# Product-key experts: 144 tokens gathered and 368 dense, with blocks of V as the stationary operand

## The chip, the core and the metric

The kernel runs on one core of one Trainium2 chip. The metric is the device time of one execution in microseconds (us), as the median of several runs. Engines are named as in the profile: PE (TensorE matmul), PEld (its weight load), DVE (VectorE), ACT (ScalarE), POOL (GpSimd) and SP (SyncE, which issues DMAs).

## The reference

One layer of a hybrid encoder block on 512 tokens of width 2048: a combined projection, neighbourhood attention beside a bidirectional RWKV-7 mixer, an output projection, and then an expert network. What matters here is the last part, all in float32:

```python
q = (u @ w_q).reshape(T, 8, 256)                       # u: the normed residual x, T = 512
s1, s2 = q[..., :128] @ sub_k1.T, q[..., 128:] @ sub_k2.T
# per head: the 16 best pairs of 128 x 128 keys -> 16 of 16384 experts, gate = softmax of their scores
hidden = gelu(einsum('cd,chkd->chk', u, exp_u[ec])) * gate      # exp_u, exp_v: 16384 x 2048
out = einsum('chk,chkd->cd', hidden, exp_v[ec])                 # 8 x 16 = 128 picks per token
x = x + gate2 * out
```

## The kernel before

The stages run one after the other: front and mixer, attention and merge (to about 1900 us), `out_proj`, `peer_select`, then `Experts.form` and `Experts.main`, which fill the time from about 2300 us to the end.

**Two ways to the experts.** For the first 128 tokens (`TS`) the kernel gathers: token t sits on partition t, and for each of its 128 picks `Picks` fetches one row of U and one of V per token (1 MB per fetch, an indirect DMA from POOL's queue into one of three `row` buffers). A row of U gives a dot product with the token (`L1221` on DVE), a row of V is added to `y3` (`L1229` on DVE). For the other 384 tokens (`TD`) the kernel computes all 16384 experts densely: U times tokens, Gelu, times a gate that is zero for experts not picked, times V.

**The dense part.** An expert tile is 128 experts. A U unit multiplies 16 blocks of U^T (128x128) with the token columns. Every float32 product is made of three float32r matmuls (`mm3`): high part of the weights by high and by low part of the tokens, low part of the weights by the high part. So a U unit is 48 matmuls of 384 columns. `Experts.spill` stores every fourth expert tile's result (32 tiles) in the forming stage; the main stage makes the other 96. A group is four expert tiles: six U steps (three units of two steps) and then eight V steps. In a V step the gated activations H are the stationary operand, 128 tokens at a time, and V streams by 512 columns: 3 token tiles x 2 expert tiles x 3 parts = 18 matmuls of 512 columns (`L1457` to `L1459`); two steps fill three PSUM tiles of [128 tokens, 512], which DVE adds to `ys` (`L1378`).

**The weight stream.** Each step needs one tile of 128x1024 weights. SP loads it into `raw` (`L1284`, two buffers), ACT casts it to the high part `wh` (`L496`), and DVE, or POOL for every `k.lp`-th tile, subtracts to get the low part `wl` (`L498`, in `w_split`); the step's matmuls follow two steps later. Here and elsewhere a helper makes the instruction, and the profile then names its line, L131: look for the tile.

**The gates.** In the forming stage `Gates` builds, in sets of 8 tokens, the gate of every expert for every dense token, and POOL stores them to `G` in blocks of 32 tokens. The main stage reads them back per group (`gt`, from SP's queue, the first from POOL's), and POOL multiplies them into the activations (`gated`, `L1352`). With `gt` a spilled tile (`ge<-gel`) is loaded.

**What sets the order.** From `form` on, each engine runs its instructions in the order in which the program writes them: per step first the split and load for two steps on, then what is late from the last unit (H parts), the unit's end (additions, gating), the matmuls, and at the end of each unit as many picks as the pace asks for. POOL's queue thus holds, in this order, gate multiplications and row fetches, and each fetch waits until DVE is done with the row it replaces.

Of the kernel before, what the change touches and what calls it, by code (L numbers as in the profile page):

```python
# [448 lines left out]
TS = 128  # L449
TD = 512 - TS  # L450
NT = TD // 128
# [546 lines left out]
def out_proj(k, tc):  # L998
    nc = k.nc
    V, A, G, T = nc.vector, nc.scalar, nc.gpsimd, nc.tensor  # L1000
    with tc.tile_pool(name="x2", reuse_waits="tile", bufs=1) as xp, tc.tile_pool(name="psE", reuse_waits="tile", bufs=1, space=PSUM) as pp:
# [5 lines left out]
        for d in range(16):  # L1007
# [31 lines left out]
        for kt in range(16):  # L1039
# [6 lines left out]
            if kt % 4 == 0:  # L1046
                pt = pp.tile([128, 512], F32, name="acc3", bufs=4)
            T.transpose(pt[:TS, (kt % 4) * 128:(kt % 4 + 1) * 128], x[:, :TS], k.c["I"])
            if kt % 4 == 3:
                A.copy(k.u3[:TS, (kt - 3) * 128:(kt + 1) * 128], pt[:TS])  # L1050


def peer_select(k, tc, pq, psF):
# [45 lines left out]
    for t in range(4):  # L1099
# [22 lines left out]
        if t == 0:  # L1122
            flat = lambda a: a[:TS].rearrange("p h n -> p (h n)")
            V.tensor_copy(k.g3[:TS], flat(sel[0]))
            V.scalar_tensor_tensor(k.idx3[:TS], flat(sel[1]), 128.0, flat(sel[2]), ALU.mult, ALU.add)
        if t < TS // 128:
            continue
        for i in range(3):
            p = psF.tile([128, 512], F32, name="sp", bufs=2)
            T.transpose(p[:, :128], sel[i].rearrange("p h n -> p (h n)"), k.c["I"])  # L1130
            A.copy(k.selT[i][:, t * 128 - TS:t * 128 + 128 - TS], p[:, :128])


class Gates:
# [35 lines left out]
    def keep(self, g):  # L1170
        if 0 <= g < self.n:
# [5 lines left out]
            if q == 3:  # L1177
                k.nc.gpsimd.dma_start(k.G[g // 4], self.st)

# [7 lines left out]
class Picks:  # L1187
# [4 lines left out]
    def __init__(self, k):  # L1192
        self.k, self.items, self.fetched, self.at = k, [], [], 0
        nb = 128 // self.BATCH
        for b in range(nb + 1):
            js = lambda i: [(i, j) for j in range(self.BATCH * (b - i), self.BATCH * (b - i + 1))]
            dots, adds = js(0) if b < nb else [], js(1) if b else []
            mix = [x for p in zip(dots, adds) for x in p] if dots and adds else dots + adds
            self.items += mix

    def fetch(self):
        k, n = self.k, len(self.fetched)
        if n < len(self.items):
            kind, j = self.items[n]
            t = k.rows.tile([128, D], F32, name="row", bufs=k.rb)
            k.nc.gpsimd.indirect_dma_start(out=t, out_offset=None, in_=k.i[("un", "vn")[kind]],  # L1206
                                           in_offset=bass.IndirectOffsetOnAxis(ap=k.idx3[:, j:j + 1], axis=0))
            self.fetched.append(t)

    def step(self):  # L1210
# [3 lines left out]
        V, A = k.nc.vector, k.nc.scalar  # L1214
# [360 lines left out]
def lay_out(i):  # L1575
# [3 lines left out]
    r = {}  # L1579
# [65 lines left out]
```

## Time and profile before

| | |
|---|---|
| runs (three) | median 4622.17 us, from 4617.81 to 4643.67 |
| the profiled execution | 4636.11 us, its span 4634.3 us |
| mean granted clock of TensorE in it | 0.969 of full speed |
| HBM | read 889.22 MB, written 88.08 MB |
| DMA queues | SP's 662.05 MB, POOL's 315.38 MB |

Busy times below are of that one execution. Matmuls are pipelined, so their durations (389 ns median for 512 columns) overlap; their pace is the distance between starts. A wait is put down to what came last; idle time of an engine that is not the bottleneck costs nothing.

### The profile page before, as it was taken

The numbers are of one execution on the slowest core, as the hardware profiler recorded it, in microseconds if no ns is written. First come the engines' busy times: TensorE is split into PE (matmuls) and PEld (weight loads), VectorE is DVE, ScalarE is ACT, GpSimd is POOL, SyncE is SP. The second block draws the span as 40 slices with busy tenths as digits, with TensorE's granted clock in tenths as the row PEclk, the third lists the DMA queues.
The fourth block names the chain that finished last, engine by engine and source line by source line (L and its number), as shares of the span: only waits on it lengthen the run. The fifth ranks groups of instructions, "written<-read, shape, count | busy, mean of one in ns | idle before, by whom it ended". The sixth has DMA issues, their size and how long they took to land.

```text
span 4634.3 us, 63846 instructions
## 1 busy us (share of the span) xinstructions
PE 4392.5 (95%) x23633; PEld 3724.2 (80%) x23633; DVE 3195.8 (69%) x4854; ACT 1757.6 (38%) x3368; POOL 1549.6 (33%) x1322
## 2 busy tenths in 40 slices
PE   6979999999999989998989999999999999999999
PEld 5757777777776777787889998888888888898887
DVE  8856665556552766546897767777777777777777
ACT  4532445454434443334246633222322232322332
POOL 4236344444432312232233322222222232322223
PEclk9989999999989989998999999999999999999999
DMA  9765344434432747652246777877777777787785
GB/s 327 245 228 162 121 132 130 114 114 117 120 86 78 263 159 243 232 182 79 91 147 244 246 261 284 283 265 282 279 269 279 279 269 283 275 287 283 270 291 170
DMA packets 371305, 981.52 MB, mean 212 GB/s; under 512 B 82416, under 2 KB 134512, under 8 KB 336432
## 3 DMA queue, kind: packets, MB, share of 16 engines
q1 hardware_dynamic: 325968, 662.05, 44.1%
q0 software_dynamic: 45024, 315.38, 18.2%
q8 instruction: 186, 3.05, 0.3%
q14 instruction: 127, 1.04, 0.1%
HBM read 889.22 MB, written 88.08 MB: 211 GB/s over the span
## 4 chain that ended last, share of the span: by engine, by line
PE 52%; DMA 18%; DVE 13%; issue 4%; ACT 4%; POOL 2%; SPq 2%; ACTq 0%; POOLq 0%; DVEq 0%
PE acc L131 35%; DMA raw<-pv 8%; DMA raw<-pu 6%; DVE wl L131 4%; PE pm L131 4%; PE acc L1459 3%; PE acc L1457 3%; ACT wh L131 3%; PE acc L1458 3%; PE us L131 2%; PE xo L131 2%; DMA adaw<-ada 1%; DVE row L1221 1%; DMA TT<-sQ 1%; PE pg L1168 1%
## 5 line engine op out<-in xcount | busy, mean ns | idle before, releaser
L131 PE MATMUL acc<-X,wh 128*128 128x384 f32 (+1 forms) x7680 | 2242.4, 369 | 23.6 <-ACT wh L131 12.8
L131 PEld LDWEIGHTS acc<-X,wh 128*128 128x128 f32 x7680 | 1413.4, 190 | 172.7 <-ACT wh L131 15.9
L131 ACT CAST wh<-raw 128x1024 fp32r<-128x1024 f32 (+1 forms) x952 | 836.0, 880 | 1691.4 <-DMA raw<-pv 557.9
L131 PE MATMUL acc<-X,wl 128*128 128x384 f32 (+1 forms) x3840 | 1418.7, 370 | 13.4 <-DVE wl L131 10.2
L131 DVE TENSOR_TENSOR wl<-raw,wh 128x1024 fp32r<-128x1024 f32 (+1 forms) x644 | 781.0, 1214 | 623.6 <-ACT wh L131 614.2
L131 PEld LDWEIGHTS acc<-X,wl 128*128 128x128 f32 x3840 | 727.8, 190 | 91.1 <-DVE wl L131 15.9
L131 POOL TENSOR_TENSOR wl<-raw,wh 128x512 fp32r<-128x512 f32 (+1 forms) x308 | 477.6, 1553 | 770.8 <-ACT wh L131 707.3
L1457 PE MATMUL acc<-wh,H 128*128 128x512 f32 x1536 | 604.7, 394 | 31.8 <-ACT wh L131 17.7
L1459 PE MATMUL acc<-wl,H 128*128 128x512 f32 x1536 | 604.6, 394 | 6.9 <-DVE wl L131 6.6
L1458 PE MATMUL acc<-wh,H 128*128 128x512 f32 x1536 | 602.3, 392 | 2.7 <-DVE H L521 2.7
L1206 POOL DMA_INDIRECT row<-un,idx x128 | 184.6, 1442 | 634.3 <-DVE y L1229 575.1
L1457 PEld LDWEIGHTS acc<-wh,H 128*128 128x128 f32 x1536 | 290.7, 189 | 103.9 <-ACT wh L131 28.1
L1206 POOL DMA_INDIRECT row<-vn,idx x128 | 182.2, 1424 | 529.6 <-DVE row L1221 492.4
L1459 PEld LDWEIGHTS acc<-wl,H 128*128 128x128 f32 x1536 | 290.6, 189 | 76.3 <-DVE wl L131 15.8
L1458 PEld LDWEIGHTS acc<-wh,H 128*128 128x128 f32 x1536 | 290.6, 189 | 62.1 <-DVE H L521 3.0
L1229 DVE SCALAR_TENSOR_TENSOR y<-row,s,y 128x2048 f32<-128x2048 f32 x127 | 297.9, 2346 | 0.0
L1221 DVE SCALAR_TENSOR_TENSOR row<-row,u 128x2048 f32<-128x2048 f32 x128 | 292.3, 2284 | 0.0
L1378 DVE TENSOR_TENSOR y<-y,acc 128x512 f32<-128x512 f32 x360 | 225.1, 680 | 0.0
L131 DVE SCALAR_TENSOR_TENSOR SVU<-us,Wc,S0w 64x64 f32<-64x64 f32 x224 | 63.4, 283 | 223.2 <-PE us L131 219.1
L1352 POOL TENSOR_TENSOR ge<-ge,gt 128x384 f32<-128x384 f32 x128 | 178.0, 1401 | 90.3 <-ACT ge L1369 75.7
L553 DVE SCALAR_TENSOR_TENSOR adacc<-adaw,sc,adacc 128x512 f32<-128x512 f32 x180 | 162.6, 903 | 47.0 <-DMA adaw<-ada 44.7
L1143 DVE TENSOR_TENSOR o<-ct,selT 128x1024 f32<-128x1024 f32 x96 | 145.3, 1540 | 37.5 <-PE pg L1168 37.2
(316 smaller groups left out, 4909.0 us busy)
## 6 DMA issues: line engine op xcount, KB each, us to landing
raw<-pu SPq DMA_DIRECT2D x256, 512.0 KB
raw<-pv SPq DMA_DIRECT2D x256, 512.0 KB
adaw<-ada SPq DMA_DIRECT2D x192, 512.0 KB
raw<-w_in SPq DMA_DIRECT2D x272, 256.0 KB
G<-st POOLq DMA_DIRECT2D x12, 2048.0 KB
gt<-G SPq DMA_DIRECT2D x31, 768.0 KB
raw<-w_ab SPq DMA_DIRECT2D x32, 512.0 KB
raw<-w_out SPq DMA_DIRECT2D x32, 512.0 KB
```

What stands on the lines that cost most here:

```text
L131: return f(*a, **kw)
L553: V.scalar_tensor_tensor(a, w[:, j], c, a, ALU.mult, ALU.add)
L1143: eng.tensor_tensor(o, in0, in1[:, t:t + 8].unsqueeze(2).to_broadcast([128, 8, 128]), op)
L1168: self.k.nc.tensor.matmul(p[:, j], o2[:, 4 * a + j], o1[:, 4 * a + j], start=True, stop=True)
L1206: k.nc.gpsimd.indirect_dma_start(out=t, out_offset=None, in_=k.i[("un", "vn")[kind]], in_offset=bass.IndirectOffsetOnAxis(ap=k.idx3[:, j:j ...
L1221: V.scalar_tensor_tensor(r, r, 1.0, k.u3, ALU.mult, ALU.mult, accum_out=k.s3[:, j:j + 1])
L1229: V.scalar_tensor_tensor(k.y3, r, k.s3[:, j:j + 1], k.y3, ALU.mult, ALU.add)
L1352: G.tensor_tensor(gv, gv, gts[g][:, :, c, :], ALU.mult)
L1378: V.tensor_tensor(y, y, acc, ALU.add)
L1457: T.matmul(acc, H[:, 0, ts], hw, start=(e == 0), stop=False)
L1458: T.matmul(acc, H[:, 1, ts], hw, start=False, stop=False)
L1459: T.matmul(acc, H[:, 0, ts], lw, start=False, stop=(e == 3))
```

## The change

`X2 = 16` more tokens are gathered, and 368 instead of 384 computed densely. The 128 picks of a token of these sixteen are spread over eight lanes of 16 partitions, so 16 more fetches of U and 16 of V serve them; a matmul with `lanes` adds the lanes at the end. In the dense part blocks of V (128 experts x 128 columns) become the stationary operand and H streams with 368 columns: a V step is 2 output blocks x 4 expert tiles x 3 parts = 24 matmuls. The result stands with output columns on partitions (16 tiles `y` of 128x368), so gate2 becomes a scalar per partition and the residual is kept in columns too (`xd`). `pv` is laid out for it. With 368 tokens the last block of gates is half full. Every fifth split of the main stage goes to POOL (`LPMAIN`), picks are paced per step and not per unit, and the forming stage takes a pick at every other set of gates and not at every third. The last U units come before V's last group but one.

```diff
-TS = 128
+X2 = 16
+TS = 128 + X2
 TD = 512 - TS
-NT = TD // 128
+NB, HB = divmod(TD, 32)
...
+            nc.gpsimd.dma_start(k.xd[d], x[:, TS:])
             if d % 4 == 3:
-                for t in range(4):
+                for t, w in ((0, 128), (1, X2)):
                     pt = pp.tile([128, 512], F32, name="acc3", bufs=4)
                     for j in range(4):
-                        T.transpose(pt[:, j * 128:(j + 1) * 128], xs[d - 3 + j][:, t * 128:(t + 1) * 128], k.c["I"])
+                        T.transpose(pt[:w, j * 128:(j + 1) * 128], xs[d - 3 + j][:, t * 128:t * 128 + w], k.c["I"])
                     xr = xp.tile([128, 512], F32, name="xr", bufs=2)
-                    A.copy(xr, pt)
-                    nc.gpsimd.dma_start(k.x2[t, :, (d - 3) * 128:(d + 1) * 128], xr)
+                    A.copy(xr[:w], pt[:w])
+                    nc.gpsimd.dma_start(k.x2[t, :w, (d - 3) * 128:(d + 1) * 128], xr[:w])
...
-            T.transpose(pt[:TS, (kt % 4) * 128:(kt % 4 + 1) * 128], x[:, :TS], k.c["I"])
+                pt = [pp.tile([128, 512], F32, name="acc3", bufs=4) for t in range(2)]
+            for t, w in ((0, 128), (1, X2)):
+                T.transpose(pt[t][:w, (kt % 4) * 128:(kt % 4 + 1) * 128], x[:, t * 128:t * 128 + w], k.c["I"])
...
+                xr = xp.tile([128, 512], F32, name="xr", bufs=2)
+                A.copy(xr[:X2], pt[1][:X2])
+                nc.gpsimd.dma_start(k.u3b[:, cs], xr[:X2])
...
+        if t == 1:
+
+            ib = pq.tile([X2, 128], I32, name="ib")
+            V.scalar_tensor_tensor(ib, flat(sel[1])[:X2], 128.0, flat(sel[2])[:X2], ALU.mult, ALU.add)
+            for a in range(128 // X2):
+                for dst, src in ((k.idx3, ib), (k.g3, flat(sel[0])[:X2])):
+                    nc.gpsimd.dma_start(dst[a * X2:(a + 1) * X2, 128:], src[:, a * X2:(a + 1) * X2])
...
                 k.nc.gpsimd.dma_start(k.G[g // 4], self.st)
+            elif g == self.n - 1:
+                for r in (slice(0, 64), slice(64, 128)):
+                    k.nc.gpsimd.dma_start(k.G[g // 4][r, :, :HB], self.st[r, :, :HB])
...
+        for lo, hi in ((0, 128), (128, 128 + X2)):
+            nb = (hi - lo) // self.BATCH
+            for b in range(nb + 1):
+                js = lambda i: [(i, lo + j) for j in range(self.BATCH * (b - i), self.BATCH * (b - i + 1))]
+                dots, adds = js(0) if b < nb else [], js(1) if b else []
+                mix = [x for p in zip(dots, adds) for x in p] if dots and adds else dots + adds
+                self.items += mix
+            self.items += [("x2", lo // 128), ("g2", lo // 128)]
...
+            if kind == "x2":
+                w = X2 if j else 128
+                k.nc.gpsimd.dma_start(t[:w], k.x2[j, :w])
+            elif kind == "g2":
+                k.nc.gpsimd.dma_start(t, k.g2r.to_broadcast([128, D]))
+            else:
+                k.nc.gpsimd.indirect_dma_start(out=t, out_offset=None, in_=k.i[("un", "vn")[kind]],
+                                               in_offset=bass.IndirectOffsetOnAxis(ap=k.idx3[:, j:j + 1], axis=0))
...
+        if kind == "g2":
+            self.finish(j, r, self.x2)
+            self.fetch()
+        elif kind == 0:
             V.scalar_tensor_tensor(r, r, 1.0, k.u3, ALU.mult, ALU.mult, accum_out=k.s3[:, j:j + 1])
             if j % self.BATCH == self.BATCH - 1:
                 cs = slice(j + 1 - self.BATCH, j + 1)
                 A.activation(k.s3[:, cs], k.s3[:, cs], AF.Gelu)
-                k.nc.gpsimd.tensor_tensor(k.s3[:, cs], k.s3[:, cs], k.g3[:, cs], ALU.mult)
-        elif j == 0:
-            V.tensor_scalar(k.y3, r, k.s3[:, 0:1], None, op0=ALU.mult)
+                G.tensor_tensor(k.s3[:, cs], k.s3[:, cs], k.g3[:, cs], ALU.mult)
+            if j == 127:
+                for a in range(128 // X2):
+                    G.dma_start(k.u3[a * X2:(a + 1) * X2], k.u3b)
+        elif j % 128 == 0:
...
+    def finish(self, j, g2, x2):
+
+        k = self.k
+        G = k.nc.gpsimd
+        if j == 0:
+            G.tensor_tensor(g2, k.y3, g2, ALU.mult)
+            G.tensor_tensor(x2, x2, g2, ALU.add)
+            G.dma_start(k.o["out"], x2)
+            return
+        for c in range(4):
+            cs = slice(c * 512, (c + 1) * 512)
+            p = self.pp.tile([128, 512], F32, name="acc5", bufs=6)
+            k.nc.tensor.matmul(p[:X2], k.lanes, k.y3[:, cs], start=True, stop=True)
+            k.nc.vector.tensor_tensor(g2[:X2, cs], p[:X2], g2[:X2, cs], ALU.mult)
+        G.tensor_tensor(x2[:X2], x2[:X2], g2[:X2], ALU.add)
+        G.dma_start(k.o["out2"], x2[:X2])
...
+LPMAIN = 5
...
-            while made < min(4 * g + 6, 128):
+            while made < (4 * g + 6 if g < 30 else 128):
...
-                if done % 3 == 2:
+                if done % 2:
                     self.picks.step()
...
-        ys = [[vp.tile([128, 512], F32, name="y%d_%d" % (t, c)) for c in range(4)] for t in range(NT)]
+        nb, ng, n = -(-TD // 32), 32, len(steps)
+        ys = [vp.tile([128, TD], F32, name="y%d" % d) for d in range(16)]
...
+                t = gts[g] = vp.tile([128, nb, 4, 32], F32, name="gt", bufs=2)
+                src = k.G.rearrange("b p i t -> p b i t")[:, :, g * 4:(g + 1) * 4]
+                by.dma_start(t[:, :NB].rearrange("p b c t -> p b (c t)"), src[:, :NB].rearrange("p b i t -> p b (i t)"))
+                if HB:
+                    by.dma_start(t[:, NB, :, :HB], src[:, NB, :, :HB])
...
-            gv = ge.rearrange("p (b t) -> p b t", t=32)
-            G.tensor_tensor(gv, gv, gts[g][:, :, c, :], ALU.mult)
+            gv = ge[:, :32 * NB].rearrange("p (b t) -> p b t", t=32)
+            G.tensor_tensor(gv, gv, gts[g][:, :NB, c, :], ALU.mult)
+            if HB:
+                gv = ge[:, 32 * NB:]
+                G.tensor_tensor(gv, gv, gts[g][:, NB, c, :HB], ALU.mult)
...
+            for j, acc in enumerate(accs.pop(("v", q))):
+                d = 4 * b + 2 * q + j
+                y, acc = ys[d], acc[:, :TD]
                 if a == 0:
                     V.tensor_copy(y, acc)
                 elif a < ng - 1:
                     V.tensor_tensor(y, y, acc, ALU.add)
                 else:
-                    o = gp.tile([128, 512], F32, name="o", bufs=2)
-                    V.tensor_tensor(o, acc, fin["g2"][:, cs], ALU.mult)
-                    V.tensor_tensor(o, o, y, ALU.add)
-                    nc.sync.dma_start(k.o["out"][t + 1, :, cs], o)
...
-            for c in range(4):
-                pt = pp.tile([128, 512], F32, name="acc5", bufs=6)
-                bcast_rows(k, pt, k.mod[:, 80 + 4 * c:84 + 4 * c])
-                A.copy(g2[:, c * 512:(c + 1) * 512], pt)
-            x2 = k.rows.tile([128, D], F32, name="row", bufs=k.rb)
-            nc.sync.dma_start(x2, k.x2[0])
-            G.tensor_tensor(k.y3, k.y3, g2, ALU.mult)
-            G.tensor_tensor(k.y3, k.y3, x2, ALU.add)
-            nc.gpsimd.dma_start(k.o["out"][0], k.y3)
...
+                    V.scalar_tensor_tensor(y, acc, k.mod[:, 80 + d:81 + d], y, ALU.mult, ALU.add)
+                    nc.sync.dma_start(k.o["outT"][d], y)
...
+            for j in range(2 * q, 2 * q + 2):
+                d = 4 * b + j
+                V.scalar_tensor_tensor(ys[d], ys[d], k.mod[:, 80 + d:81 + d], fin[b % 2][:, j], ALU.mult, ALU.add)
...
+        k.lp = LPMAIN
...
-                if q == 0:
-                    accs["v"] = [pp.tile([128, 512], F32, name="acc5", bufs=6) for t in range(NT)]
-                two.append((h, l))
-                if m >= n - 2:
-
-                    order = [(t, e) for t in range(NT) for e in range(4)] if q else []
-                else:
-                    order = [(t, 2 * q + j) for j in range(2) for t in range(NT)]
-                for t, e in order:
-                    acc = accs["v"][t]
-                    hw, lw = (x[:, e % 2 * 512:(e % 2 + 1) * 512] for x in two[e // 2])
-                    H = hs[4 * a + e]
-                    ts = slice(t * 128, (t + 1) * 128)
-                    T.matmul(acc, H[:, 0, ts], hw, start=(e == 0), stop=False)
-                    T.matmul(acc, H[:, 1, ts], hw, start=False, stop=False)
-                    T.matmul(acc, H[:, 0, ts], lw, start=False, stop=(e == 3))
-                if q:
-                    two.clear()
-            if q == 1:
-                ended = kind, a, b
-                while picks.at < len(picks.items) and picks.at < early + todo * (m + 1 - first) // (pace - first):
-                    picks.step()
-        unit_done(*ended)
+                h, l = ws.pop(m)
+                accs["v", q] = [pp.tile([128, 512], F32, name="acc5", bufs=6) for j in range(2)]
+                for j, acc in enumerate(accs["v", q]):
+                    for e in range(4):
+                        w = slice(e * 256 + j * 128, e * 256 + j * 128 + 128)
+                        mm3(k, acc, h[:, w], l[:, w], hs[4 * a + e], e == 0, e == 3, slice(0, TD))
+            ended = steps[m]
+            if picks.at < len(picks.items) and picks.at < early + todo * (m + 1 - first) // (pace - first):
+                picks.step()
+        step_done(*ended)
...
-    r["pv"] = i["peer_v"][0].reshape(32, 2, 2, 128, 4, 512).transpose(0, 4, 1, 3, 2, 5).reshape(32, 8, 128, 1024)
+    r["pv"] = i["peer_v"][0].reshape(32, 4, 128, 8, 256).transpose(0, 3, 2, 1, 4).reshape(32, 8, 128, 1024)
```

## Rows read from the trace of the kernel before

**Rows 1.** The page, part 1: busy time, share of the span, instructions.
```profile
PE 4392.5 (95%) x23633; PEld 3724.2 (80%) x23633; DVE 3195.8 (69%) x4854; ACT 1757.6 (38%) x3368; POOL 1549.6 (33%) x1322
```

**Rows 2.** Stretches: length, busy PE/PEld/DVE/ACT/POOL, PE clock, DMA share, GB/s.
```profile
2470.00:2680.00 210.00, 199.70 (x1327) 198.62 (x1326) 158.40 (x114) 139.98 (x338) 78.90 (x58) 0.98 0.70 247
2748.00:4520.00 1772.00, 1730.88 (x8501) 1536.02 (x8499) 1317.20 (x1240) 524.13 (x649) 505.06 (x379) 1.00 0.79 278
```

**Rows 3.** Chain of waits, 3990 to 4135 us: start, length, what.
```profile
3992.21 24.98 PE acc L131 x144
...
4049.88 24.98 PE acc L131 x144
...
4107.55 24.98 PE acc L131 x144
```

**Rows 4.** Line 1457 in two windows: ns min/median/max, first and last start.
```profile
L1457 PE MATMUL acc<-wh,H x48: 387/389/500, 2806.0 to 2840.9; 128*128 128x512 f32 x48
...
L1457 PE MATMUL acc<-wh,H x48: 387/389/390, 4487.3 to 4519.3; 128*128 128x512 f32 x48
```

**Rows 5.** Waits from 2740 to 4560 us: total, times, longest.
```profile
ACT wh L131 <- DMA raw<-pv: 537.5, 175, 11.4
...
ACT wh L131 <- DMA raw<-pu: 400.8, 129, 9.2
...
ACT wh L131 <- PE acc L131: 83.2, 33, 4.5
...
PEld acc L1457 <- ACT wh L131: 28.1, 18, 4.5
```

**Rows 6.** Chain of waits, 3085 to 3126 us.
```profile
3103.62 0.43 SPq L1344
...
3104.99 14.50 DMA raw<-pv
...
3119.59 1.05 ACT wh L131
```

**Rows 7.** Groups from 2740 to 4560 us: busy us, mean ns, idle before.
```profile
L131 DVE TENSOR_TENSOR wl<-raw,wh 128x1024 fp32r<-128x1024 f32 x424 | 547.9, 1293 | 456.7 <-ACT wh L131 450.6 <-PE acc L1459 1.7 <-PE acc L131 1.6
...
L1229 DVE SCALAR_TENSOR_TENSOR y<-row,s,y 128x2048 f32<-128x2048 f32 x121 | 283.8, 2346 | 0.0
...
L1221 DVE SCALAR_TENSOR_TENSOR row<-row,u 128x2048 f32<-128x2048 f32 x116 | 264.9, 2284 | 0.0
L1378 DVE TENSOR_TENSOR y<-y,acc 128x512 f32<-128x512 f32 x348 | 217.6, 680 | 0.0
...
L1397 POOL TENSOR_TENSOR y<-y,row 128x2048 f32<-128x2048 f32 x1 | 4.6, 4614 | 3.0 <-DMA row<-x 3.0
```

**Rows 8.** Tile wl in the forming stage, 2400 to 2740 us.
```profile
L131 POOL TENSOR_TENSOR wl<-raw,wh x13: 2366/2501/3038, 2427.4 to 2660.9; 128x1024 fp32r<-128x1024 f32 x13
```

**Rows 9.** Line 1413, the additions at the end.
```profile
L1413 DVE TENSOR_TENSOR y<-y,row x6: 679/1773/1783, 4564.6 to 4584.3; 128x512 f32<-128x512 f32 x6
```

**Rows 10.** Tile acc from 2740 us: last U and last V matmuls.
```profile
L1459 PE MATMUL acc<-wl,H x1536: 387/389/796, 2748.8 to 4628.0; 128*128 128x512 f32 x192
L131 PE MATMUL acc<-X,wl x1473: 334/334/447, 2739.9 to 4587.6; 128*128 128x384 f32 x185
```

**Rows 11.** Chain of waits from 4587 us to the end.
```profile
4621.51 2.99 DMA out<-o
```

**Rows 12.** Order of time on PE, 2099 to 2103 us.
```profile
2099.71 1.99 PE L1022 MATMUL acc<-ct,x 128*128 128x128 f32 x16
```

**Rows 13.** Line 1025, the stores of x in the out projection.
```profile
L1025 POOL DMA_DIRECT2D x<-xr x16: 542/543/582, 1961.2 to 2108.6; - x16
```

**Rows 14.** Order of time on POOL, 2680 to 2830 us.
```profile
2695.38 0.59 POOL L1178 DMA_DIRECT2D G<-st  x1 [4.65 <-ACT st L1176]
...
2710.83 1.05 POOL L1344 DMA_DIRECT2D gt<-G  x1 [2.52 <-issue]
2716.68 1.82 POOL L1206 DMA_INDIRECT row<-vn,idx  x1 [4.79 <-DMA gt<-G]
```

More of the change, by code (lines that the diff above doesn't have):

```diff
@@ L1193, in __init__ @@
         self.k, self.items, self.fetched, self.at = k, [], [], 0
[L1194 to L1199, printed above, removed]
+        for lo, hi in ((0, 128), (128, 128 + X2)):
[6 more added lines that the diff above has]
+            self.items += [("x2", lo // 128), ("g2", lo // 128)]
     def fetch(self):
@@ L1335, in main @@
         V, A, G, T = nc.vector, nc.scalar, nc.gpsimd, nc.tensor
-        nb, ng, n = TD // 32, 32, len(steps)
-        ys = [[vp.tile([128, 512], F32, name="y%d_%d" % (t, c)) for c in range(4)] for t in range(NT)]
+        nb, ng, n = -(-TD // 32), 32, len(steps)
+        ys = [vp.tile([128, TD], F32, name="y%d" % d) for d in range(16)]
         hs, gts, ges, accs = {}, {}, {}, {}
-        late, two = [], []
+        late = []
+        picks.pp = pp
         def gates_of(g, by=nc.sync):
             if g < ng:
-                gts[g] = vp.tile([128, nb, 4, 32], F32, name="gt", bufs=2)
-                by.dma_start(gts[g].rearrange("p b c t -> p b (c t)"),
-                                  k.G.rearrange("b p i t -> p b (i t)")[:, :, g * 128:(g + 1) * 128])
+                t = gts[g] = vp.tile([128, nb, 4, 32], F32, name="gt", bufs=2)
[3 more added lines that the diff above has]
+                    by.dma_start(t[:, NB, :, :HB], src[:, NB, :, :HB])
         def gated(e):
@@ L1359, in parts @@
             def parts():
-                hs[e] = vp.tile([128, 2, TD], F32R, name="H", bufs=6)
+                hs[e] = vp.tile([128, 2, TD], F32R, name="H", bufs=8)
                 split_to(k, hs[e], ge)
@@ L1404, in fetch_columns @@
+                    nc.sync.dma_start(k.o["outT"][d], y)
+        fin = []
         def fetch_columns(c):
+            if c == 0:
+                for t in (k.rows.tile([128, D], F32, name="row", bufs=k.rb), k.u3):
+                    fin.append(t[:, :4 * TD].rearrange("p (d t) -> p d t", d=4))
             if c < 4:
-                nc.sync.dma_start(fin["x2"][c % 2], k.x2.rearrange("t p d -> p t d")[:, 1:, c * 512:(c + 1) * 512])
-        def finish_columns(c):
-            cs = slice(c * 512, (c + 1) * 512)
-            for t in range(NT):
-                G.tensor_tensor(ys[t][c], ys[t][c], fin["g2"][:, cs], ALU.mult)
-                V.tensor_tensor(ys[t][c], ys[t][c], fin["x2"][c % 2][:, t], ALU.add)
-            fetch_columns(c + 2)
+                nc.sync.dma_start(fin[c % 2], k.xd.rearrange("d p t -> p d t")[:, 4 * c:4 * c + 4])
@@ L1427, in main @@
             done = ended
-            if ended:
-                unit_done(*ended)
-                ended = None
+            if done:
+                step_done(*done)
+                if done[0] == "v" and done[1] == ng - 2:
+                    late.append(lambda d=done[2:]: finish_columns(*d))
             if m == n - 20:
                 assert picks.at == len(picks.items)
-                finish_start()
-            if done and done[0] == "v" and done[1] == ng - 2:
-                late.append(lambda c=done[2]: finish_columns(c))
-            h, l = ws.pop(m)
+                fetch_columns(0)
+                fetch_columns(1)
             if kind == "u":
@@ L1558, in build @@
             k.u3 = k.sp.tile([128, D], F32, name="u3")
-            k.g3 = k.sp.tile([128, 128], F32, name="g3")
-            k.idx3 = k.sp.tile([128, 128], I32, name="idx3")
+            k.g3 = k.sp.tile([128, 128 + X2], F32, name="g3")
+            k.idx3 = k.sp.tile([128, 128 + X2], I32, name="idx3")
             k.wn, k.whb = 1024, 3
@@ L1639 @@
     ins = {n: nc.dram_tensor(n, a.shape, mybir.dt.from_np(a.dtype), kind="ExternalInput").ap() for n, a in arrays.items()}
-    outs = {"out": nc.dram_tensor("out", (4, 128, 2048), F32, kind="ExternalOutput").ap()}
+    shapes = {"out": (128, 2048), "out2": (X2, 2048), "outT": (16, 128, TD)}
+    outs = {n: nc.dram_tensor(n, s, F32, kind="ExternalOutput").ap() for n, s in shapes.items()}
     with tile.TileContext(nc, schedule_with_timeline_sim=True) as tc:
@@ L1643 @@
     r = _run(nc, [arrays], core_ids=[0])
-    return np.asarray(r.results[0]["out"]).reshape(1, 512, 2048)
+    o = {n: np.asarray(r.results[0][n]) for n in shapes}
+    return np.concatenate([o["out"], o["out2"], o["outT"].reshape(2048, TD).T])[None]
```

65 lines of the change are left out of this document (33 added, 32 removed).

## The prediction

> **What bounds the kernel now.** The page comes first: TensorE is busy for 95% of the span, the next engine, DVE, for 69% [rows 1]. The table of stretches then says where to look: in the long main stage (2748 to 4520 us) PE is busy for 1731 of 1772 us, at full clock, while DVE has 1317, POOL 505 and the DMA engines a share of 0.79 [rows 2]. A busy PE is not yet a PE at its peak, so I look for its pace. The chain of waits shows U blocks of 144 matmuls of 384 columns in 24.98 us, and three of them start 57.67 us apart with nothing but matmuls between [rows 3]. That gives clean prices: 24.98/144 = 173.5 ns for 384 columns and (57.67 - 24.98)/144 = 227.0 ns for the 512 of the V block between. One group (six U steps, eight V steps) costs 57.67 us where nothing stands in its way. What a group costs on average, the first starts of line 1457 in two windows say: V block 1 begins at 2806.0, V block 29 at 4487.3, so 1681.3/28 = 60.05 us [rows 4]. PE loses 2.38 us per group, 67 us over these 28.
>
> The waits tell to what. PE waits for ACT's casts of the weights; but ACT waits for raw weights to land, 537.5 + 400.8 us, against 83.2 us for PE's U matmuls to give a buffer back [rows 5]. So the weight stream (two raw tiles, each loaded, cast, split, then loaded again) runs at about PE's own pace and seldom has to wait for PE. One V block shows a loss: gt is loaded ahead of a V tile on SP's queue, that tile takes 14.50 us to land, and its cast starts only then [rows 6]. The kernel is bound by PE, with a weight stream close behind.
>
> **The change part by part.** *Matmuls.* Two prices 128 columns apart give (227.0 - 173.5)/128 = 0.418 ns a column, and 173.5 - 384 x 0.418 = 13 ns that each matmul costs beside. No row shows 368 columns; 173.5 bounds them above, 173.5 x 368/384 = 166.3 below, and the line through both prices gives 173.5 - 16 x 0.418 = 166.8 ns, which I take. U has 32 x 48 = 1536 matmuls in the forming stage and 96 x 48 = 4608 in the main one: 6.7 ns less each is 10.3 and 30.9 us. V has 32 x 144 = 4608 of 512 columns (1046.0 us) and gets 32 x 192 = 6144 of 368 (1024.8 us): 21.2 us less. So the main stage saves 52 us of PE work, and a clean group costs 336 x 166.8 = 56.0 us. In the forming stage PE is busy for 200 of 210 us [rows 2], but eight more gathered rows (8 x 2.3 us on DVE) enter it, against two steps of gates fewer; I count half, -5 us, bounds -13 and +8.
>
> The Trainium skill, TensorE: Matmul & The Clock Gate (Back-to-back issue gap), has N/2.4 + 2.5 ns for a warm matmul. By that V would go from 994 to 957 us, 16 us better than the 21 above; the rows have 13 ns where it has 2.5, and they decide.
>
> *The gathered tokens.* The 128 picks of each of the sixteen tokens are spread over eight lanes, so there are 16 + 16 row operations more (288 for 256). The main stage gets 264 instead of 240: 24 x 2.32 us [rows 7] is 56 us more on DVE, and 25 MB more of loads, 5% of the 493 MB that 278 GB/s move in 1772 us [rows 2]. The y additions go from 384 of 512 columns at 0.68 us [rows 7] to 512 of 368; between 0.49 (in proportion) and 0.68 I take 0.55, +21 us. Every fifth split goes to POOL: 89 x 1.29 = 115 us off DVE [rows 7]. DVE ends 38 us lighter, so its new work costs nothing while its idle quarter lasts. That cover is thinnest in a V step: 2 x 1.29 + 3 x 0.68 + 1.13 x 2.32 = 7.2 of 8.2 us for two steps now, 0.8 x 1.29 + 2 x 0.55 + 0.63 x 2.32 = 3.6 of 4.0 then.
>
> *The split on POOL and the lost time.* In the forming stage such a split takes 2.50 us on POOL [rows 8], 1.2 more than on DVE. In POOL's queue it stands behind the fetch of the last pick, which waits until DVE is done with a row; late are then the raw buffer, the load into it, and at last PE's weights. Rows also load oftener: the DMA share grows to some 0.79 x 1.05 x 60/58.5 = 0.85, and a step has (57.67 - 56.0)/14 = 0.12 us less to hide a load in. Against this stands a more even order: at most one pick per step (now two together at times), and two additions in each V step instead of three in every other, so that fewer row loads fall on the same moment as gt and ge. The 67 us of lost PE time may shrink by 10 or grow by 100; I take +20, a third of today's loss more: late splits and heavier loads press on the V steps that already stall, and nothing in the rows presses on the others.
>
> *The end.* Now POOL multiplies y by gate2 while DVE adds: such additions take 1773 ns instead of 679 [rows 9]. The last V block runs from 4587.6 to 4628.0 [rows 10], 40.4 us for a clean 32.7, and the last additions wait for output buffers, 2.99 us at one place [rows 11]. After the change one DVE operation finishes a block and y itself is stored. -8 for the block, -2 for the tail; bounds 0 and -13.
>
> *Out projection.* 64 transposes become 32; 16 take 1.99 us [rows 12], and three of the four groups lie in PE's way: 3 x 1 us, and a little of the wait for their evictions, -4. In the norm loop ACT gets four more copies and POOL's queue four DMAs of 0.54 us [rows 13] between its multiplications: +2, at most +6.
>
> *Small work on POOL.* Indices and weights of the lanes are 16 DMAs, 16 x 0.54 = 9 us in the selection, ahead of splits that POOL does there: +4, bounds 0 and 9. The half block of gates is stored in 16384 runs of 64 bytes. The store of a whole block takes POOL 0.59 us, the first gt, with 1536 runs, 1.05 [rows 14]; at 0.5 ns a run the two halves take 4 us each. Their landing is not shown, and POOL already waits 4.79 us for the first gt [rows 14], so a delay is soon felt: +5, bounds 0 and 30. In mid-stage POOL gets two multiplications like the one of 4.61 us [rows 7] and eight loads of u3, which can each hold up a split: +4, bounds 0 and 9. PE has four float32 matmuls of 512 columns for the lanes: +3.
>
> *Sum:* -52 - 5 + 20 - 10 - 4 + 2 + 4 + 5 + 4 + 3 = -33 us. The profiled execution (span 4634.3, time 4636.1 us) would become 4603. The median of the runs lies 14 us below it; the same -33 there gives 4589, **4590 us**.
>
> **Rivals.** *Evenness wins* (27%). Lost PE time shrinks by 10 us instead of growing by 20: 4589 - 30 = 4559 us. For it: two groups in a row pass without any loss [rows 3]. Against it: the stream must then keep up with 56.0 us, with more rows beside it.
>
> *The weight stream paces the main stage* (20%), and the change doesn't do what it says. PE is faster but gets its weights at the old 60 us a group: all 52 us of saved PE work turn into waiting, not 20 of them, 4589 + 32 = 4621 us. For it: ACT's 938 us of waiting for landings against 83 for PE [rows 5]. Against it: groups of 57.67 us, at which the stream kept up.
>
> *POOL's splits come late* (18%), the case on the other side. Place: POOL's queue, a split behind a fetch that waits for DVE. Price: 1.2 us longer and 1 to 3 us of queue at 89 tiles, 200 to 370 us; two raw tiles take turns, so half of it falls on the stream, and PE's buffers hide a part. It decides once a split is later than what a V step has to spare, nothing in blocks that already stall. With +90 instead of +20 of lost time: 4659 us. Rows 9 speak for it too: a DVE addition stands still while POOL multiplies [rows 9]. Against it, the gathers' row operations with POOL at work beside them keep a mean of 2.28 and 2.35 us [rows 7]. The Trainium skill, SBUF — State Buffer (Who interferes with whom), says that DVE instructions with two SBUF inputs and GpSimd instructions that read SBUF lock each other out for the whole instruction; by that rule 89 splits of 2.5 us would close the port for 222 us. The additions agree, the row operations show nothing of it.
>
> **How the numbers follow.** The forecast has 35%, the rivals 27, 20 and 18. Half a percent, 23 us, is about what a measurement of this kernel can tell (the runs before lie 26 us apart). Faster, below 4599: the first rival and most of the forecast's cases, 0.55. Same: 0.25, the second rival and the forecast's slower cases. Slower, above 4645: the third rival and a bad end of the second, 0.20. The range takes in the first rival and the third: 4540 to 4660.
>
> **What would show it.** Matmuls of 368 columns 166 to 168 ns apart; group starts 56.0 us apart where nothing stalls and about 59 on average; splits on POOL at 2.5 us, and if they end over 4 us behind their cast, the third rival is at work. ACT's wait for landings against its wait for PE tells whether the stream paces. The last V block should take 32 us. I am wrong if groups stay at 60 us, or if the first V block starts late for want of gates.

## The result, and the profile after

The change makes the kernel slower: 4741.31 us in the median of 4 runs (4731.49 to 4744.09) against 4626.28 us for the kernel before beside it, a ratio of 1.024 with a 95% interval of 1.0206 to 1.0274. The forecast was 4590, the range ended at 4660. In the profiled execution the span grew from 4634.3 to 4738.4 us.

The page, part 1, and the stretch 2860 to 4360 us (length, busy PE/PEld/DVE/ACT/POOL, PE clock, DMA share, GB/s) of the changed kernel:

```profile
PE 4385.9 (93%) x25113; PEld 3880.1 (82%) x25113; DVE 3314.8 (70%) x4934; ACT 1743.2 (37%) x3352; POOL 1894.1 (40%) x1614
...
2860.00:4360.00 1500.00, 1377.08 (x7900) 1347.34 (x7899) 1119.14 (x1046) 415.68 (x522) 651.60 (x499) 0.97 0.79 277
```

In the main stage PE is now busy for 92% of the time, where [rows 2] had 98%. No engine took its place: DVE has 75%, POOL 43%, and the DMA engines move 277 GB/s at a share of 0.79, as before. The matmuls themselves are about as fast as forecast; tile acc in three windows (ns min/median/max, first and last start):

```profile
L131 PE MATMUL acc<-H,wh x104: 327/331/644, 2793.7 to 2830.0; 128*128 128x368 f32 x104
...
L131 PE MATMUL acc<-X,wh x96: 327/330/332, 3793.7 to 3817.3; 128*128 128x368 f32 x96
...
L131 PE MATMUL acc<-H,wh x112: 327/331/531, 4596.5 to 4629.7; 128*128 128x368 f32 x112
```

The clean U block in the middle goes from 3793.7 to the next V block at 3817.7: 24.01 us for 144 matmuls, 166.7 ns each. But V block 1 begins at 2793.7 and V block 29 at 4596.5, so a group takes 1802.8/28 = 64.39 us where it took 60.05 [rows 4]. No V block here runs without a loss; in the experiment with three buffers and the splits on DVE, below, they take 32.32 us (168.3 ns a matmul) and start 56.33 us apart. So 8.06 us are lost in each group, for 2.38 before. Over 28 groups the longer group is 121.5 us; the first V block starts 16.3 us earlier than before, the way from V block 0 to 1 is 4.1 us longer and that from block 29 to the end 5.1 us shorter: 121.5 - 16.3 + 4.1 - 5.1 = 104.2, the whole difference of the spans.

The waits between 2740 and 4640 us (total, times, longest):

```profile
ACT wh L131 <- DMA raw<-pv: 525.1, 154, 8.9
ACT wh L131 <- DMA raw<-pu: 460.0, 144, 7.5
...
ACT H L521 <- POOL ge L1415: 138.1, 63, 15.6
PEld acc L131 <- POOL wl L131: 91.2, 56, 13.0
PE acc L131 <- DVE y L1442: 82.8, 30, 7.2
ACT wh L131 <- PE acc L131: 76.7, 22, 6.4
PE acc L131 <- POOL wl L131: 73.9, 51, 12.7
```

PE waits 74 us for low parts from POOL, which is new, and 83 us for DVE's additions. (The 91 us of PE's weight load for low parts lie over the same stretches; the 165 us named in the expectation of the first experiment count them twice.) Behind both, as the experiments with a third buffer show, stands the first pair: ACT waits 985 us for raw weights to land and 77 us for PE. The steps of that wait, one after the other, in order of time (the lines of SP's queue from windows of their own, since it joins issues of one kind):

```profile
3306.86 0.38 SPq L1341 DMA_DIRECT2D raw<-pv  x1
...
3309.52 0.33 SPq L1341 DMA_DIRECT2D raw<-pv  x1
...
3314.07 1.05 ACT L131 CAST wh<-raw 128x1024 fp32r<-128x1024 f32 x1 [5.46 <-DMA raw<-pv]
...
3315.20 2.34 POOL L131 TENSOR_TENSOR wl<-raw,wh 128x1024 fp32r<-128x1024 f32 x1 [1.50 <-PE acc L131]
3315.43 1.04 ACT L131 CAST wh<-raw 128x1024 fp32r<-128x1024 f32 x1
3315.55 2.39 DVE L522 TENSOR_TENSOR H<-ge,H 128x368 fp32r<-128x368 f32 x1 [3.11 <-ACT H L521]
...
3317.57 0.33 SPq L1341 DMA_DIRECT2D raw<-pv  x1
...
3318.54 0.78 PE L131 MATMUL acc<-H,wh 128*128 128x368 f32 x2 [3.22 <-DVE y L1442]
3318.76 2.28 DVE L1253 SCALAR_TENSOR_TENSOR row<-row,u 128x2048 f32<-128x2048 f32 x1
3320.97 1.22 DVE L131 TENSOR_TENSOR wl<-raw,wh 128x1024 fp32r<-128x1024 f32 x1
...
3322.22 0.33 SPq L1341 DMA_DIRECT2D raw<-pv  x1
...
3325.52 1.05 ACT L131 CAST wh<-raw 128x1024 fp32r<-128x1024 f32 x1 [3.49 <-DMA raw<-pv]
```

The load of 3306.86 is cast at 3314.07, that of 3309.52 at 3315.43. POOL's low part ends at 3317.54, and 0.03 us later the load that needs its raw buffer is asked for. The next cast ends at 3316.47, but its low part starts only at 3320.97: DVE is at H (2.39 us beside POOL's split; the median of all is 0.54), two additions and a row operation first. It ends at 3322.19, the load follows at 3322.22, its cast starts at 3325.52 after waiting. Two buffers take turns in this loop, so **two weight steps take as long as one load and one split together**. For the steps with casts between 2800 and 4350 us, averaged from the starts and ends of loads, casts and low parts in each trace (the load from its asking to the start of its cast, the split from that start to the end of the low part):

```
                                  load to   cast to end  end to     two    x 7    group
                                  cast      of low part  next load  steps  =      measured
before                            5.71      2.77         0.09       8.57   60.0   60.05 us
change                            5.40      3.55         0.18       9.13   63.9   64.39
change, splits on DVE             5.77      3.01         0.14       8.92   62.4   62.52
before, with POOL's splits        5.44      3.23         0.14       8.81   61.7   61.65
before, with 33 more rows         6.08      2.90         0.13       9.11   63.8   63.96
change, one set, splits on DVE    5.49      2.79         0.16       8.44   59.1   59.17
```

That the three parts add up to the steps holds for any buffer used in turn. What they tell is that a freed buffer is asked for at once and that its load is then waited for: little in this loop stands idle for PE's sake. It paced the kernel before as well, at 60.05 us and not at PE's 57.67; the third buffer, below, is the test of that.

Not all of the 8.06 us is standing. PE's waits between 2740 and 4640 us come to some 165 us, 5.6 a group; the rest is pace. After the wait of 3.22 us that ends at 3318.54, the granted clock from 3318.6 to 3322.1 us is 0.52, close to the 1.2 GHz level, and V matmuls start 0.31 us apart; from 3322.2 to 3326 it is 1.00 and they start 0.17 us apart. From 2860 to 4360 us the granted clock has a mean of 0.97, where [rows 2] had 1.00 for the main stage. With a third buffer it is 1.00 and the waits are nearly gone. What the lower clock cost by itself was not tested.

### The profile page after: what moved, and what is told of

It is laid out like the page before. It is cut to its first block, busy times and chain, and to the rows that moved or that the text cites. A ratio compares the mean times of both kernels' runs of the same rounds, so it can differ in the third digit from the quotient of the medians.

```text
span 4738.4 us, 67546 instructions
## 1 busy us (share of the span) xinstructions
PE 4385.9 (93%) x25113; PEld 3880.1 (82%) x25113; DVE 3314.8 (70%) x4934; ACT 1743.2 (37%) x3352; POOL 1894.1 (40%) x1614
## 5 line engine op out<-in xcount | busy, mean ns | idle before, releaser
L131 PE MATMUL acc<-X,wh 128*128 128x368 f32 (+1 forms) x7680 | 2231.8, 369 | 19.7 <-ACT wh L131 12.4
L131 PE MATMUL acc<-X,wl 128*128 128x368 f32 (+1 forms) x3840 | 1419.4, 370 | 44.1 <-POOL wl L131 36.1
L131 PE MATMUL acc<-H,wh 128*128 128x368 f32 x4096 | 1051.3, 339 | 85.1 <-DVE y L1442 82.8
L131 POOL TENSOR_TENSOR wl<-raw,wh 128x512 fp32r<-128x512 f32 (+1 forms) x397 | 703.6, 1774 | 850.7 <-ACT wh L131 766.4
L131 PEld LDWEIGHTS acc<-H,wh 128*128 128x128 f32 x4096 | 746.0, 193 | 99.2 <-issue 55.2
L131 PE MATMUL acc<-H,wl 128*128 128x368 f32 x2048 | 691.9, 338 | 52.3 <-POOL wl L131 49.5
L131 PEld LDWEIGHTS acc<-H,wl 128*128 128x128 f32 x2048 | 395.3, 193 | 63.9 <-POOL wl L131 59.4
L1442 DVE TENSOR_TENSOR y<-y,acc 128x368 f32<-128x368 f32 x480 | 233.7, 531 | 0.0
L1412 POOL TENSOR_TENSOR ge<-ge,gt 128x352 f32<-128x352 f32 x128 | 168.6, 1317 | 82.9 <-ACT ge L1433 66.5
L131 DVE TENSOR_TENSOR M<-Q,MT 128x8 f32<-128x8 f32 (+14 forms) x240 | 122.7, 511 | 7.9
```

Source lines behind the costliest of these rows:

```text
L131: return f(*a, **kw)
L1412: G.tensor_tensor(gv, gv, gts[g][:, :NB, c, :], ALU.mult)
L1442: V.tensor_tensor(y, y, acc, ALU.add)
```

## The experiments

All runs stand beside runs of the kernel before on the same chip. Medians, ratios to the kernel before, and groups (as in rows 4, from V blocks 1 and 29):

```
                                     us        ratio [95% interval]      group
change, splits on DVE                4699.74   1.0169 [1.0152, 1.0186]   62.52
before, with POOL's splits           4697.10   1.0153 [1.0119, 1.0187]   61.65
change, one set                      4654.37   1.0075 [1.0057, 1.0093]   60.96
change, one set, splits on DVE       4593.78   0.9926 [0.9906, 0.9946]   59.17
 (of the change, splits on DVE:)
 + each ninth gather light           4669.59   1.0095 [1.0058, 1.0132]   62.27
 + each ninth row operation light    4696.88   1.0167 [1.0133, 1.0202]   62.37
 + both                              4662.06   1.0080 [1.0047, 1.0113]   62.15
 + later gathers                     4713.83   1.0179 [1.0139, 1.0219]   63.18
 + third raw buffer                  4527.24   0.9783 [0.9749, 0.9817]   56.67
before, with 33 more rows            4763.18   1.0297 [1.0274, 1.0320]   63.96
before, third raw buffer             4580.04   0.9898 [0.9863, 0.9932]   57.67
change, third raw buffer             4529.37   0.9785 [0.9759, 0.9811]   57.14
before, 33 more rows, third buffer   4589.93   0.9929 [0.9901, 0.9957]   57.71
```

**The change without splits on POOL.**

```diff
-LPMAIN = 5
+LPMAIN = 0
```

> The changed kernel with one number altered: in the main stage no part of the weight splits goes to GpSimd (LPMAIN 0 in place of 5), VectorE does all of the low part as in the kernel before. Theory 1 (the splits on GpSimd cost the time: their parts come late, the gate multiplications queue behind them, and they hold the port that VectorE's row operations need): the group of 14 weight steps falls from 64.4 us to 57 to 60 us, the whole to 4560 to 4620 us, and TensorE's waits on a low part written by GpSimd, some 165 us between 2730 and 4640, are gone; VectorE's row operations go back from a mean of 2.5 us to 2.35. Rival (the order with blocks of V stationary, or the 12% of further gathered rows, costs it): the group stays at 62 us or more and the whole within 1% of 4741 us, the same time then standing under waits on VectorE or on the weight loads.

42 us of the 115 come back, not all, and the group stays over the 62 us named for the rival: the waits for POOL's low parts are gone, and the group still takes 62.52 us.

**The kernel before with POOL's splits.**

```diff
         gates_of(0, nc.gpsimd)
+        k.lp = 5
```

> The kernel before with the one number alone: in its main stage every split gives the share that the change gives (5 in place of 0) to GpSimd. Theory 1: slower than the kernel before by 50 to 150 us, its group of 14 steps goes from 60.05 us to 62 to 65 us, and TensorE starts to wait on low parts from GpSimd. Rival (the order or the further rows cost the time, GpSimd's part is harmless): within 0.5% of the kernel before, or some 10 us faster since VectorE is given 1 us a step.

71 us slower than the kernel before beside it. The splits cost time in either order; the group of 61.65 us is just under the 62 to 65 expected.

**The change without the second set of rows.**

```diff
-        for lo, hi in ((0, 128), (128, 128 + X2)):
+        for lo, hi in ((0, 128),):
```

> The changed kernel without the second set of gathered rows: the 16 further tokens' 32 row operations, their two late loads of the gathered tokens' inputs and the matmuls that add the lanes are left out, and these tokens' output is their residual input alone, so the sum over experts of 16 tokens is missing. GpSimd keeps its share of the splits. Rival 2 (the further row gathers crowd the weight stream and VectorE): the group falls to 58 to 61 us and the whole to 4560 to 4640 us. Theory 1: 32 of some 220 row operations less give back at most 12% of the loss, 4700 to 4735 us, and the waits on GpSimd's parts stay above 120 us.

87 us below the change: more than the theory of the splits allows, yet with 4654 us above the 4560 to 4640 of the other, and above the kernel before.

**Both edits: no splits on POOL, no second set.**

> Both edits: no split on GpSimd in the main stage, and the second set of gathered rows left out (the sum over experts of 16 tokens is missing). Theory 1: 10 to 30 us below the run with the first edit alone, since 32 row operations of 2.3 us leave VectorE. Rival 2: the same as the run without the second set alone, 4560 to 4640 us. If the order with V stationary costs the time: neither edit helps, over 4680 us.

148 us below the change and 32 us below the kernel before (with the experts of 16 tokens left out): both causes are real, and the order with V stationary without them is no loss. 106 us separate it from the run with the splits on DVE and both sets. Next question: what do 32 row operations cost it by?

**Light gathers, light row operations, both.** One of nine places; the third run has both edits.

```diff
+            elif n % 9 == 4:
+                k.nc.gpsimd.dma_start(t[:, :64], k.x2[0, :, :64])
...
+        w = slice(0, 64 if self.at % 9 == 4 else D)
```

> The changed kernel with VectorE doing all the splits of the main stage (as in the first run) and each ninth row gather (32 of 288, as many as the second set has) replaced by a load of 64 columns; the row operation behind it stays as long and reads a tile that lies in SBUF, so these rows' contribution to the output is left out. It takes away the bytes of 32 gathers and keeps VectorE's work. If the gathers' bytes cost the time (weights and rows together move 275 to 282 GB/s between 2800 and 4400 in every kernel so far, before, after and without the second set): 80 to 120 us below the first run's 4700, so 4580 to 4620. If VectorE's row operations cost it: within 25 us of 4700.

> The counterpart: all splits on VectorE, every gather whole, but each ninth row operation of VectorE works on 64 columns in place of 2048, so most of these rows' contribution is left out. It takes 32 operations of 2.4 us (77 us) from VectorE and keeps the bytes. If VectorE's work costs the time: 60 to 110 us below 4700, so 4590 to 4640. If the bytes cost it: within 25 us of 4700.

> All splits on VectorE, two raw buffers, and at the same 32 of 288 places both reductions: a load of 64 columns in place of the gather and a row operation on 64 columns (these rows' contribution is left out). The places themselves, their issue on GpSimd and their order stay. If gathers and operations lengthen the loop of two buffers together (the one hides what the other gives back): 80 us or more below 4700, near the 4594 of the run that left the places out. If the places cost the time (their issue and their order in the queues): 4640 to 4700, no more than the sum of the two single runs, 30 and 3 us below.

30, 3 and 38 us below 4700, each uncertain by some 20 us. Neither the bytes nor DVE's time is what the rows cost by itself, and the two together give about their sum. (The first of these expectations quotes 275 to 282 GB/s for every kernel so far; two of them, the change with one set and the kernel before with POOL's splits, moved 270.)

**Later gathers.**

```diff
-        while len(self.fetched) < k.rb:
+        while len(self.fetched) < min(len(self.items), self.at + k.rb - (self.items[self.at][0] == "g2")):
             self.fetch()
...
-        self.fetch()
```

> All splits on VectorE, two raw buffers, and a gather asked for at the step after the row operation that frees its buffer, so that GpSimd's queue no longer stands still behind VectorE (in the first run it waited 837 us for row operations between 2800 and 4400) with the gate multiplications behind it. If that queue is the part of the loss that neither the bytes nor VectorE's time carried alone: 40 us or more below 4700. If not: within 25 us of 4700, or slower where VectorE then waits for rows.

4714 us: nothing came back, though between 2860 and 4360 us, against the change with splits on DVE, POOL's waits for row operations fell from 759 to 573 us and ACT's for the gated H from 100 to 69. A quarter less of POOL's standing still gained nothing. That speaks against it as the cause, but three quarters of it were left, so it is not ruled out as a part.

**More rows in the kernel before.**

```diff
+            self.items += [(2, max(b - 1, 0))]
...
+        elif kind == 2:
+            V.scalar_tensor_tensor(r, r, 1.0, k.u3, ALU.mult, ALU.mult, accum_out=k.sx)
```

> The kernel before, its order and tiles untouched, with 33 further row gathers and as many further row operations (on VectorE, their result unused) mixed into its 256: what the second set adds, without the change's order. If the further rows are what costs the change its time: 80 to 120 us slower than the kernel before, 4700 to 4745. If it is the order with the blocks of V stationary that can't bear them: 0 to 40 us slower.

140 us slower, more than the 80 to 120 expected, in the old order: the rows cost at least as much there.

**A third raw buffer, in four kernels.** The edit is the same in all; the kernel before gives up one of two output buffers for the room, the changed kernel packs its gate tile.

```diff
-            self.raws[m] = k.W.tile([128, 1024], F32, name="raw", bufs=k.rawb)
+            self.raws[m] = (k.vp if k.vp and m % 3 == 2 else k.W).tile([128, 1024], F32, name="raw", bufs=1 if k.vp and m % 3 == 2 else 2)
...
+        k.vp = vp
+        load(first + 4)
...
-            load(m + 2 + k.rawb)
+            load(m + 3 + k.rawb)
```

> All splits on VectorE and, in the main stage, three buffers for the raw weight steps in place of two, each load asked for one step earlier (the gate tile is packed to make room). If the time is lost because a weight load waits for the split that frees its buffer (a loop of latencies, not a limit of bytes or of VectorE): 60 us or more below 4700. If bytes or VectorE set the pace: within 25 us of 4700, the loads merely waiting elsewhere.

> The kernel before with a third buffer for the raw weight steps in its main stage, each load asked for one step earlier (one output buffer of the last group is given up for the room). Theory of the loop (two buffers: a load is asked for 0.03 us after the low part of the split that frees its buffer ends; load 5.71 us + split 2.77 us + 0.09 us make 8.57 us for two steps, 4.29 us a step, and 14 steps are the group's 60.05 us): with three buffers the group falls to its clean 57.7 us, 60 us less in all, 4555 to 4585. The run of the change with three buffers (4527) then lies 30 to 60 us below it, which is the gain in columns and ends that was forecast. If the loop held only the change: within 20 us of 4623.

> The change with its splits on GpSimd as they are (5) and the third raw buffer. If the splits cost time only by lengthening the loop of two buffers (cast to end of the low part 3.55 us against 3.01 without them): within 25 us of the 4527 of the run without them. If late low parts and a held-up GpSimd queue cost by themselves: 4560 or more, with TensorE's waits on GpSimd's low parts still above 80 us.

> The kernel before with the 33 further gathers and row operations (140 us slower than the kernel before with two raw buffers) and the third raw buffer. Theory of the loop: the rows cost time only by stretching the loop, so with three buffers it comes within 25 us of the same kernel without the rows. If the rows are too much for the bytes or for VectorE: 60 us or more above it.

This settles that the loop of two buffers is what turns splits and rows into lost time. With three buffers the splits on POOL cost 2 us in place of 42, the 33 rows 10 us in place of 140 (each uncertain by some 20 us), and the kernel before falls to the 57.67 us a group that its matmuls need. The stretch 2860 to 4360 us and the waits in it, of the kernel before with the third buffer:

```profile
2860.00:4360.00 1500.00, 1500.00 (x7493) 1353.12 (x7492) 1147.88 (x1090) 460.17 (x571) 431.20 (x335) 1.00 0.81 289
...
ACT wh L131 <- PE acc L1461: 544.2, 192, 3.0
ACT wh L131 <- PE acc L131: 316.7, 119, 3.2
ACT wh L131 <- DMA raw<-pv: 45.8, 14, 5.9
```

And of the change with it, splits on POOL as they were:

```profile
2860.00:4360.00 1500.00, 1485.13 (x8820) 1481.04 (x8819) 1274.46 (x1169) 463.45 (x579) 777.69 (x555) 1.00 0.87 310
...
ACT wh L131 <- PE acc L131: 494.9, 212, 4.2
...
ACT wh L131 <- DMA raw<-pu: 99.6, 26, 5.4
ACT wh L131 <- DMA raw<-pv: 80.7, 32, 5.7
...
PEld acc L131 <- POOL wl L131: 14.3, 8, 8.4
PE acc L131 <- POOL wl L131: 11.9, 7, 8.1
```

PE is busy for 1500 and 1485 of 1500 us. ACT now waits for PE, so the stream runs ahead. The DMA engines move 310 GB/s at a share of 0.87 and DVE is busy for 85%: at 277 GB/s and 75% neither had been at a limit. The two runs of the change with three buffers, 4527 and 4529 us, are 2.2% below the kernel before and 4.5% below the change.

## Why the prediction was wrong

*Right or nearly so:* the price of a matmul (166.8 ns forecast; 166.7 in U blocks, 168.3 in V blocks) and with it the clean group (56.0; 56.33), and the low part on POOL (2.50 us; mean 2.58). At the end, the last two V blocks take 64.8 us, 32.4 each, and the tail behind them 3.7 us, where the last block took 40.4 and the tail 5.9 before: the -8 and the -2 came as forecast. Yet from block 29 on only 5.1 us were gained, for these 10 and what the columns were to give. Up to the first V block the sum had +2 and the change was 16.3 us ahead; but the experiments that keep the change's code up to there start that block between 2726.4 and 2745.6, so little of this is sure. The two halves of the last gate block take POOL 2.69 us each, not 4 (rows 14 would have given 0.3 ns a run, (1.05 - 0.59)/1536, and not 0.5), and the first V block is not late. For a 368-column matmul the rule of the Trainium skill weighed in the prediction (TensorE: Matmul & The Clock Gate, Back-to-back issue gap) would give an estimate of 155.8 ns; the trace has 166.7, and it decides.

*The step that failed* is "The split on POOL and the lost time": +20 us, bounds -10 to +100. It measured (8.06 - 2.38) x 28 = +159 us. With that in place of +20 the sum comes to +106, near the 104 by which the spans differ. Two things went into it that the sum had elsewhere or at nothing.

First, the reading behind it. From ACT's 938 us of waiting for landings [rows 5] the prediction concluded a stream "at about PE's own pace", and from DVE's idle quarter that its new work "costs nothing". The loop shows that the stream already set the 60.05 us. Idle time on DVE is no cover for work that stands in front of a low part in its queue: in the loop every such delay is passed on to the load behind it, and half of it to each step. So the second set, whose 24 row operations in the main stage and gathers were priced at zero, costs 87 us with the splits on POOL and 106 without (these runs leave out its finish too); 33 more rows cost 140 in the old order.

Second, the size of the splits' part. They cost 42 us with both sets and 61 with one, 71 in the old order. The mechanism is that of the third rival: the low part on POOL ends 4.08 us behind its cast on average (66 of them between 2860 and 4360, 32 of them over 4), just past the 4 us that the prediction named as its sign. Its price, 70 us more of lost time than in the sum, is at the upper end of what the splits cost; its condition, that a split decides "nothing in blocks that already stall", was wrong: in the loop a late buffer adds to whatever else is late. Without the second set and the splits the change is worth -32 us (4593.78 against 4625.93), with the experts of 16 tokens left out.

*The second rival* had the right sign, waiting for landings against waiting for PE, but took the pace of the stream as fixed at 60 us. It is no rate but a sum of latencies, and the change lengthened it by 0.56 us for two steps.

*The finish of the first set* was in the sum with +4 for POOL's two operations and eight loads. One V block took 50.31 us around it, for a clean 32.32 and a mean of 38.7:

```profile
4386.43 4.63 POOL L1272 TENSOR_TENSOR row<-y,row 128x2048 f32<-128x2048 f32 x1
...
4387.04 4.43 DVE L522 TENSOR_TENSOR H<-ge,H 128x368 fp32r<-128x368 f32 x1 [0.65 <-ACT H L521]
...
4391.14 4.70 POOL L1273 TENSOR_TENSOR row<-row 128x2048 f32<-128x2048 f32 x1
4391.39 6.60 DVE L1253 SCALAR_TENSOR_TENSOR row<-row,u 128x2048 f32<-128x2048 f32 x1
...
4402.52 2.35 POOL L131 TENSOR_TENSOR wl<-raw,wh 128x1024 fp32r<-128x1024 f32 x1
...
4404.92 0.68 PE L131 MATMUL acc<-H,wl 128*128 128x368 f32 x1 [12.66 <-POOL wl L131]
```

DVE's two operations take 4.43 and 6.60 us for some 0.5 and 2.28. They end 0.41 and 2.15 us after POOL's beside them, about their own length, as if each ran only when POOL was done. The low part on POOL then stands behind three row fetches (4398.28 to 4402.50), and PE stands for 12.66 us.

*What the rest is worth* shows where nothing waits for the loop: the change with three buffers is 4529.37 us against 4580.04 of the kernel before with three. From V block 29 to the end the latter takes 160.2 us, 13 more than the kernel before, and DVE waits 21.4 us there for stores, having one output buffer instead of two (5.0 in the kernel before). Less these 13, the change gains some 38 us. The sum's -33 held +20 of lost time; here (57.14 - 56.33) x 28 = 23 us are lost, so the other terms were near.

*Open:* how the rows' cost divides. Lighter gathers and lighter operations gave back 38 of the 106 us that leaving the places out gave. By the table of the loop the second set adds 0.28 us to the load (5.77 against 5.49) and 0.22 to the split (3.01 against 2.79) for two steps; with both made lighter the load has 5.63 and the split 3.05, so the split stays long. That the loop turns the places into lost time is shown by the third buffer; whether it is their order in the queues, the finish between the sets (52.9 us for one V block of the change with splits on DVE, in a mean of 38.4) or something else was not tried further.

## What to carry to other kernels

Where a buffer is loaded, used and loaded again, add up its loop (load asked for to landing, landing to last use, last use to next load), divide by the number of buffers and compare that with the step of the engine you think is the bound, before counting idle time on the engines in the loop as cover. If the loop is the longer one, work moved onto any engine in it costs time however idle that engine is, and faster matmuls give nothing; another buffer may be worth more than the change. An engine's mean wait for landings says that a stream is waited for, not that it keeps up.

## What the runs showed of the hardware

In this kernel DVE and POOL hold each other up for whole instructions, in small operations too. Groups of the changed kernel between 2740 and 4640 us (busy, mean ns, idle before):

```profile
L1264 DVE SCALAR_TENSOR_TENSOR y<-row,s,y 128x2048 f32<-128x2048 f32 x130 | 336.1, 2586 | 0.0
L1253 DVE SCALAR_TENSOR_TENSOR row<-row,u 128x2048 f32<-128x2048 f32 x127 | 319.9, 2519 | 0.0
...
L1415 POOL TENSOR_TENSOR ge<-ge,gt 128x16 f32<-128x16 f32 x117 | 112.8, 964 | 0.0
```

Before, they had means of 2346 and 2284 ns [rows 7], which the prediction took as a sign against this. The gate multiplication of 16 columns takes POOL 0.22 us at 2705.15 and 2.27 us at 3300.27, while DVE's row operation beside it takes 3.04 us from 3299.42. This is what the Trainium skill, SBUF — State Buffer (Who interferes with whom), states of DVE instructions with two SBUF inputs beside GpSimd instructions that read SBUF, and here the trace agrees. It cost little once the loop had a third buffer: the same operations then have means of 2582 and 2503 ns between 2860 and 4360 us with splits on POOL, in a kernel of 4529 us.

A gate store in runs of 64 bytes takes POOL 2.69 us for half of the partitions; a store of a whole block takes 0.58 us (lines 1195 and 1192).
